# Sums of w_out's blocks split into two parts beside the first gate units and fetched as parts, and one merged block's pooled rows in natural order

## The chip, the cores and the metric

The kernel runs on one core of one Trainium2 chip. Its time is the device time of one execution in microseconds (us); of several runs the median counts. One further execution was profiled, and every duration below comes from that one.

## The reference

One layer of a hybrid encoder block on x of shape (1, 1024, 1024), everything in float32. Cut to what the change touches:

```python
h = rmsnorm(x, norm_mix)
q, k, v, r, lr_f, lr_b, u, g_a, g_b = split(h @ w_in)
o = bidirectional_gated_linear_attention(q, k, v, lr_f, lr_b)      # 4 heads, chunks of 64
y_a = (o * silu(r)) @ w_branch_gla
pooled = multiscale_pool(u)                  # windows 2/4/8/16, mean minus token
y_b = einsum('blgc,gcd->blgd', pooled, w_pool_group) * pool_scale
merged = sigmoid(g_a) * y_a + sigmoid(g_b) * y_b
x = x + merged @ w_out                       # w_out is 1024 x 1024
gate, up = split(rmsnorm(x, norm_ffn) @ w_ffn_in)
x = x + (silu(gate) * up) @ w_ffn_out
return rmsnorm(x, norm_final)
```

## The kernel before

**Arithmetic.** A float32 matrix is held as two parts: a high part, which is a copy rounded to the matmul's input type `fp32r` (`nc.scalar.copy`, on ScalarE: "the cast"), and a low part, the matrix minus its high part (a subtraction on VectorE or GpSimd). A product is three matmuls: high by high, high by low, low by high (`mm3`, the matmuls of L279). The cast with the subtraction is "a split" (`split_to`, L200 and L201). The large matrices are cut in 2 x 2 blocks of 512 and multiplied by a scheme of seven products, p = 1 to 7, in place of eight; some of its factors are blocks and the others are sums or differences of blocks, which other engines form ahead of TensorE. Names end in h and l for the parts: wh/wl of a weight, dh/dl of data.

**Stages.** In order of time: projections and attention (to about 340 us); eleven *gate units* (about 340 to 552), each 256 output columns of w_in times h by seven products of 12 matmuls, of the kinds r (one unit), u (two, the pool input), a and b (four each, the merge gates); the branch product y_a (about 552 to 630); the merged product with w_out (about 630 to 705); the feed-forward stages (to 1318).

**Gate units.** The loop over `gate_runs` runs the unit's products one by one; before each, `gates_ahead.step()` issues what a later product's weights need: a sum of blocks (`fs`, VectorE, L1104), the cast (`wh`, ScalarE, L200) and the subtraction (`wl`, GpSimd, L201). The results are taken from the accumulators by copies on ScalarE (L1492) and adds on VectorE (L1497); for a and b units a sigmoid follows (L1505). For each b unit a small matmul adds the pooling branch (`yb`), and a `scalar_tensor_tensor` on VectorE multiplies it with the gate. The 1024 tokens are held in two halves by parity. The kinds u and r write their rows in natural token order, by reading the accumulator through `sorted_` and writing through `halves`; a and b leave them in the permuted order. a's gates and b's rows go out to HBM (`sa_out`, `yb_out`).

**Work beside the gate units.** `prepare_beside` hangs a generator, `beside`, to the product loop, which advances it by time. Each turn of it does one job in three ages: the job's own operation (`op`, L724), the cast of the job that came `lag` turns earlier (`uph`, L718), and the subtraction of the one cast before that (`upl` on VectorE, L709); a result is written to HBM `put` turns later. At the start of unit 1 it gets `output_jobs`: for each of w_out's four strips of 128 rows it loads the four blocks and forms four differences on GpSimd, which go to `t_wo[p]` in HBM for the products p = 4, 5, 6, 7, unsplit. From unit 8 on it prepares the first two FFN units (`unit_jobs`), whose sums are cast and subtracted there and written as parts (`u_out`). The core of `beside`:

```python
            if differ:
                src, (hi, lo), dst = differ
                nc.vector.tensor_tensor(lo, src, as_f32(hi), op=ALU.subtract)       # L709
            ...
            if cast:
                parts = parts_for(src)
                nc.scalar.copy(parts[0], src)                                       # L718
                differ = src, parts, dst
            ...
                if op:
                    op()                                                            # L724
```

**Branch and merged products.** `line` lists their pieces, two halves c of the inner dimension for each product, with 24 matmuls in a piece. A piece is a triple of functions (`load`, `sums`, `make`): load fetches the raw weights (`wraw`), sums forms the data's sums, make splits data and weights. `project` runs them ahead of the piece that TensorE is at: before each piece it calls `line_load`, `line_make` and `line_sums` once each. The merged products run in the order `MERGED` = 1, 4, 6, 7, 5, 2, 3; in 4, 6, 7 and 5 the weights are the sums from `t_wo`. As the branch products finish, `merge` multiplies their results with the gates and adds the pooled rows (L1624 loads both); for block (1, 1), which comes with branch product 7, that last sum is `padd` on GpSimd (L1639).

**What sets the order.** Every engine runs its instructions in the order written. SyncE issues the loads and stores one after the other, and one that waits for its buffer holds those behind it. Buffers come from pools in turns: six each for wh and wl (`wts`; a piece takes two of each), five for the temporary tiles (`tmp`: the sums' raw strips, uph and upl, the pooling's rows).

Of the kernel before, what the change touches and what calls it, by code (L numbers as in the profile page):

```python
# [10 lines left out]
F32 = mybir.dt.float32  # L11
# [6 lines left out]
P = 128  # L18
# [4 lines left out]
HALF = 512  # L23
# [30 lines left out]
def kernel(  # L54
# [537 lines left out]


    s_out = {p: dram.tile([P, 4, HALF], F32, name=f"s_out{p}") for p in (3, 5, 6, 7)}
    t_wo = {p: dram.tile([P, 4, HALF], F32, name=f"t_wo{p}") for p in (4, 5, 6, 7)}
    READY = 2
    f_order = [f for q in range(PAIRS) for f in (q, q + PAIRS)]
    u_out = [{p: dram.tile([P, 2, HALF], F32, name=f"u_out{n}_{p}") for p in range(1, 8)} for n in range(READY)]
# [31 lines left out]
    def output_jobs(k):  # L630
        (b11, b12, b21, b22), loads = rows_of(w_out, k)
        yield from loads
        for dst, a, b, p in ((b11, b12, b11, 5), (b12, b22, b12, 7), (b22, b22, b11, 6), (b21, b21, b22, 4)):
            yield partial(psub, dst, a, b), None, t_wo[p][:, k, :]

    def unit_jobs(n):
        raw = [slot(F32, (KT, P), "fraw")[:, :, :] for _ in range(2)]
# [653 lines left out]
    def line_load():  # L1291
        if len(loads) < len(line):
            loads.append(line[len(loads)][0]())

    def line_sums():
        if len(begun_sums) < len(line):
            begun_sums.append(line[len(begun_sums)][1]())

    def line_make():
        n = len(made)  # L1300
        if n < len(line):
            while len(loads) <= n:
                line_load()
            if len(begun_sums) <= n:
                while len(begun_sums) <= n:
                    line_sums()
                settle()
            made.append(line[n][2](loads[n]))

    def weight_load(src):  # L1310
        raw = slot(s="wraw")
        nc.sync.dma_start(raw[:, :, :], src)
        return raw

    def weight_split(raw):
        parts = []
# [66 lines left out]
    def merged_piece(p, c):  # L1383
        def load():
            if p in WEIGHT_B:
                i, j = WEIGHT_B[p]
                return weight_load(chunk(w_out, i, j, c))
            return weight_load(t_wo[p][:, 2 * c : 2 * c + 2, :])

        def sums():  # L1390
            def block(i, j):
                return merged[i, j][c][:, :, :]

            if p == 6:
                s3s.append(slot(s="s3"))
                sub(s3s[c][:, :, :], block(0, 0), block(1, 0))
                padd(block(1, 0), block(1, 0), block(1, 1))
                soon(4, partial(sub, block(0, 0), block(1, 0), block(0, 0)))
            elif p == 3:
                sub(block(0, 1), block(0, 1), block(0, 0))  # L1400

        def make(raw):
            a = s3s[c] if p == 7 else merged[{1: (0, 0), 6: (0, 0), 5: (1, 0), 4: (1, 1), 2: (0, 1), 3: (0, 1)}[p]][c]
            return data_split(a, 3.5 if p == 3 else 2), weight_split(raw)

        return load, sums, make

    line += [merged_piece(p, c) for p in MERGED for c in range(2)]

# [53 lines left out]
    class Gates:  # L1463
# [7 lines left out]
        def row(self, i):  # L1471
            while len(self.rows) <= i:
                self.rows.append(slot(s="ga"))
            return self.rows[i]

        def run(self, p):
            while len(right.get(p, ())) < 2:
                next(aside[0][0])
            ps = bank_of(self, p)
            product(self.unit, p, ps, right)  # L1480
            ps = ps[:, :]
            if self.kind in "ur":
                ps = sorted_(ps)
            finish_late()

            def row(i, half):
                t = self.row(i)[:, half, :]
                return halves(t) if self.kind in "ur" else t

            part = {1: (0, 0), 6: (0, 1), 5: (1, 1)}.get(p)  # L1490
            if part:
                nc.scalar.copy(row(*part), ps)  # L1492
                return
            i, half = {2: (0, 0), 3: (0, 1), 4: (1, 0), 7: (1, 1)}[p]
            done = row(i, half)
            if p != 4:
                add(done, ps, done)  # L1497
                ps = done
            if self.kind == "r":
                if p == 4:  # L1500
                    nc.scalar.copy(done, ps)
                late.append(partial(gated, KT - 2 + i, half, done))
                return
            if self.kind != "u":
                nc.scalar.activation(done, ps, AF.Sigmoid)  # L1505
            elif p == 4:
                nc.scalar.copy(done, ps)
            self.done.append((i, half))
            if self.kind == "b" and p in (7, 4):
                for at in self.done:  # L1510
                    self.pooling(*at)
                self.done = []

        def pooling(self, i, half):
            yb = bank(ps_g, "yb")
            mm3(
                yb[:, :], tuple(t[:, i * P : (i + 1) * P] for t in wpool[self.at]),
                tuple(t[:, half, :] for t in pools[self.at]), True, True,
            )
            j, row = 2 * self.at + i, self.row(i)[:, half, :]  # L1520
            late.append(partial(
                nc.vector.scalar_tensor_tensor, row, yb[:, :], g_pool[:, j : j + 1], row, op0=ALU.mult, op1=ALU.mult
            ))

        def store(self, i):
# [14 lines left out]
    for n, run in enumerate(gate_runs):  # L1540
        zs[n] = Gates(n)
        last = n == len(gate_units) - 1
        if n == 1:
            prepare_beside(map(output_jobs, range(4)), 2.8)
        if n == 8:
            finish_side()
            finish_beside()
            prepare_beside(map(unit_jobs, range(READY)), 2.8, 0, 2)
        for at, (of, p) in enumerate(run):
            if not gates_ahead.step() and at in (5, 7):  # L1550
                line_make()
            zs[of].run(p)
            for _ in range(2 * (at == 0 < n and not last)):
                gunits[n + 1].load()
            if p in (7, 4):
                zs[of].store(int(p == 4))
            if at == 4:
                flush()
                if n == 3:
                    begin(pooling(), 4)  # L1560
            if 6 <= n < 10 and at == 5:
                load_pool_weights(n - 6)
            elif n >= 7 and at == 2:
                split_pool_weights(n - 7)
            if n >= 7 and at == (0 if last else 2):
                load_pooled(n - 7)
            if last and at == 1:
                finish_beside()
                load_block(0, 0)
                line_load()  # L1570
                line_load()
                load_block(1, 0)
            elif last and at == 2:
                line_load()
                line_load()
                load_block(0, 1)
                load_block(1, 1)
# [6 lines left out]
    def project(base, products, collect, before, amid=None, first=FIRST, up=UP, pools_of=lambda p: U_BANKS if p == 1 else X_BANKS):  # L1584
        banks = {}
        for at, p in enumerate(products):
            before(p)
            if p in first:
                banks[p in up] = [bank(pool) for pool in pools_of(p)]
            sums = banks[p in up]  # L1590
            for c in range(2):
                n = base + 2 * at + c
                settle()
                while len(made) <= n:
                    line_make()
                    settle()
                line_load()
                line_make()
                line_sums()
                if c == 1 and amid:  # L1600
                    amid(p)
                a, b = made[n]
                for m in range(4):
                    for k in range(2):
                        mm3(
                            sums[m][:, :], tuple(t[:, m * P : (m + 1) * P] for t in a[k]), b[k],
                            c == 0 and k == 0 and p in first, c == 1 and k == 1, p not in first,
                        )
                    if c == 1:
                        collect(p, m, sums[m][:, :])  # L1610
# [17 lines left out]
    def merge(i, j, m, ps, s):  # L1628

        if m == 0:  # L1630
            merged[j, i] = [slot(s="mg") for _ in range(2)]
        dst = quarter(merged[j, i], m)
        sa, yb = (quarter(t, m) for t in gates[i, j])

        if (i, j) == (1, 1):
            dst = halves(dst)
            add(dst, sorted_(ps), sorted_(s))
            nc.vector.tensor_tensor(dst, dst, sorted_(sa), op=ALU.mult)
            padd(dst, dst, sorted_(yb))  # L1639
            return  # L1640
        if s is not None:
            add(ps, ps, s)
        nc.vector.tensor_tensor(ps, ps, sa, op=ALU.mult)
        add(halves(dst), sorted_(ps), sorted_(yb))
# [511 lines left out]
```

## Time and profile before

| what | us |
| --- | --- |
| median of 3 runs | 1325.61 |
| the three runs | 1326.76, 1325.61, 1324.41 |
| the profiled execution | 1323.53 |
| its span (first to last instruction) | 1321.8 |
| TensorE's granted clock, share of full speed | 0.999 |

The busy time of each engine by stage in that execution, from the view by windows:

| from, to (us) | stage | TensorE | VectorE | ScalarE | GpSimd | DMA share | GB/s |
| --- | --- | --- | --- | --- | --- | --- | --- |
| 340.0 to 366.5 | first gate units | 25.82 | 20.60 | 14.57 | 16.22 | 0.76 | 244 |
| 366.5 to 416.3 | gate units beside w_out's sums | 49.80 | 18.22 | 19.22 | 47.77 | 0.79 | 262 |
| 416.3 to 552.0 | the other gate units | 135.70 | 101.67 | 68.33 | 83.97 | 0.81 | 268 |
| 552.0 to 629.7 | branch products | 75.93 | 64.90 | 41.23 | 59.57 | 0.85 | 324 |
| 629.7 to 705.5 | merged products | 73.52 | 59.43 | 37.50 | 51.99 | 0.34 | 117 |

In the profile's rows PE is TensorE (PEld its weight loads), DVE VectorE, ACT ScalarE, POOL GpSimd, SP SyncE. A row of the timeline reads: start, duration, engine, line, operation, result<-operands, and in brackets the idle time before it with what ended it. Matmuls are pipelined, so that their durations overlap; where TensorE stands is read from the distance of their starts. A group of instructions in a row is marked x and its count, and its duration is that of the whole group.

### The profile page before, as it was taken

The numbers are of one execution on the slowest core, as the hardware profiler recorded it, in microseconds if no ns is written. First come the engines' busy times: TensorE is split into PE (matmuls) and PEld (weight loads), VectorE is DVE, ScalarE is ACT, GpSimd is POOL, SyncE is SP. The second block draws the span as 40 slices with busy tenths as digits, with TensorE's granted clock in tenths as the row PEclk, the third lists the DMA queues.
The fourth block names the chain that finished last, engine by engine and source line by source line (L and its number), as shares of the span: only waits on it lengthen the run. The fifth ranks groups of instructions, "written<-read, shape, count | busy, mean of one in ns | idle before, by whom it ended". The sixth has DMA issues, their size and how long they took to land. (4 is left out here: it accounts for less than half of the span.)

```text
span 1321.8 us, 17901 instructions
## 1 busy us (share of the span) xinstructions
PE 1302.2 (99%) x6310; PEld 1138.0 (86%) x6310; DVE 838.3 (63%) x1034; ACT 645.3 (49%) x1177; POOL 769.0 (58%) x557
## 2 busy tenths in 40 slices
PE   9999999999999999999999999999999999999998
PEld 7888888899888888888888888888888888888886
DVE  6975556554735876778884856566666657354375
ACT  7366766665534545554347633333333334454353
POOL 3332734132598657669675286777766778465454
PEclk9999999999999999999999999999999999999999
DMA  7231623134778678996516355555444457995562
GB/s 236 104 104 42 198 75 117 59 101 128 239 247 283 195 223 303 380 409 212 185 65 240 127 189 186 183 183 173 155 142 159 150 160 257 382 349 201 182 223 80
DMA packets 167835, 251.97 MB, mean 191 GB/s; under 512 B 11161, under 2 KB 94145, under 8 KB 167745
## 3 DMA queue, kind: packets, MB, share of 16 engines
q1 hardware_dynamic: 167600, 250.57, 55.8%
q8 instruction: 49, 0.80, 0.3%
q14 instruction: 42, 0.34, 0.1%
q10 hardware_dynamic: 144, 0.26, 0.1%
HBM read 168.74 MB, written 82.05 MB: 190 GB/s over the span
## 5 line engine op out<-in xcount | busy, mean ns | idle before, releaser
L201 POOL TENSOR_TENSOR wl<-fs,wh 128x512 fp32r<-128x512 f32 x124 | 190.7, 1543 | 138.8 <-ACT wh L200 80.9
L279 PE MATMUL ps<-gh,wh 128*128 128x512 f32 x616 | 234.4, 381 | 0.5 <-DVE sums L1880 0.3
L279 PE MATMUL ps<-gl,wh 128*128 128x512 f32 x616 | 233.6, 379 | 0.7 <-DVE gl L1713 0.7
L279 PE MATMUL ps<-gh,wl 128*128 128x512 f32 x616 | 233.5, 379 | 0.0
L201 POOL TENSOR_TENSOR wl<-fraw,wh 128x512 fp32r<-128x512 f32 x93 | 131.1, 1410 | 58.0 <-ACT wh L200 52.8
L201 POOL TENSOR_TENSOR ol<-gor,oh 128x1024 fp32r<-128x1024 f32 (+1 forms) x42 | 103.2, 2462 | 76.0 <-ACT oh L200 63.1
L279 PE MATMUL ps<-hh,wh 128*128 128x512 f32 x356 | 141.1, 396 | 0.7 <-ACT ga L1492 0.7
L279 PE MATMUL ps<-hh,wl 128*128 128x512 f32 x356 | 134.9, 379 | 0.0
L279 PE MATMUL ps<-hl,wh 128*128 128x512 f32 x356 | 134.9, 379 | 0.0
L279 PEld LDWEIGHTS ps<-gh,wh 128*128 128x128 f32 x616 | 116.5, 189 | 17.9 <-DVE sums L1880 0.7
L279 PEld LDWEIGHTS ps<-gl,wh 128*128 128x128 f32 x616 | 116.4, 189 | 17.4 <-DVE gl L1713 1.1
L279 PEld LDWEIGHTS ps<-gh,wl 128*128 128x128 f32 x616 | 116.4, 189 | 16.5
L279 PE MATMUL ps<-oh,oh 128*128 128x512 f32 x308 | 116.8, 379 | 0.2 <-DVE g L1886 0.2
L279 PE MATMUL ps<-ol,oh 128*128 128x512 f32 x308 | 116.7, 379 | 0.0
L279 PE MATMUL ps<-oh,ol 128*128 128x512 f32 x308 | 116.7, 379 | 0.0
L201 POOL TENSOR_TENSOR wl<-wraw,wh 128x512 fp32r<-128x512 f32 x56 | 91.4, 1663 | 38.3 <-ACT wh L200 36.2
L201 POOL TENSOR_TENSOR wl<-raw,wh 128x512 fp32r<-128x512 f32 x34 | 47.0, 1392 | 103.2 <-ACT wh L200 70.3
L201 DVE TENSOR_TENSOR ol<-wor,oh 128x1024 fp32r<-128x1024 f32 (+1 forms) x42 | 66.6, 1601 | 62.6 <-ACT oh L200 55.1
L200 ACT CAST wh<-fs 128x512 fp32r<-128x512 f32 x124 | 75.8, 612 | 25.7 <-DVE fs L1104 23.8
L279 PEld LDWEIGHTS ps<-hh,wl 128*128 128x128 f32 x356 | 67.3, 189 | 9.6
L279 PEld LDWEIGHTS ps<-hh,wh 128*128 128x128 f32 x356 | 67.4, 189 | 9.3 <-ACT ga L1492 1.1
L279 PEld LDWEIGHTS ps<-hl,wh 128*128 128x128 f32 x356 | 67.4, 189 | 8.4
(281 smaller groups left out, 3059.4 us busy)
## 6 DMA issues: line engine op xcount, KB each, us to landing
fraw<-in_w_ffn_in_dram SPq DMA_DIRECT2D x44, 512.0 KB, 5.9
gor<-g_out SPq DMA_DIRECT2D x35, 512.0 KB, 5.7
fraw<-in_w_in_dram SPq DMA_DIRECT2D x22, 512.0 KB, 6.1
g_out<-s SPq DMA_DIRECT2D x44, 256.0 KB, 2.4
wor<-t_out SPq DMA_DIRECT2D x20, 512.0 KB, 4.2
raw<-in_w_in_dram SPq DMA_DIRECT2D x36, 256.0 KB, 5.2
g_out<-g SPq DMA_DIRECT2D x33, 256.0 KB, 2.6
x<-in_x_dram SPq DMA_DIRECT2D x16, 512.0 KB, 5.2
```

What stands on the lines that cost most here:

```text
L200: nc.scalar.copy(hi, src)
L201: eng.tensor_tensor(lo, src, as_f32(hi), op=ALU.subtract)
L279: nc.tensor.matmul(ps.rearrange("p (c a) -> p c a", a=2), a, b.rearrange("p (a c) -> p c a", a=2), **flags)
```

## The change

Three parts:

1. The sums of w_out's blocks are split where they are made. `output_jobs` now hands `beside` the sum as something to cast: behind each of the 16 sums on GpSimd come a cast on ScalarE (L718) and a subtraction on VectorE (L709), and both parts are written to `t_wo`, whose tiles have room for two. That makes 32 writes of 256 KB in place of 16. The call takes `put` = 0: a turn's writes are issued at its end, not three turns later; `lag` stays 1.
2. Merged products 4, 6, 7 and 5 fetch the parts: `line_fetch` and `weight_parts` load each piece's two wh and two wl tiles straight from `t_wo`, 32 loads of 256 KB in place of 8 of 512 KB into wraw, 16 casts on ScalarE and 16 subtractions on GpSimd. The fetch of a piece is called behind the make of the piece before it, where the raw load of before stood four pieces ahead.
3. The rows that `merge` adds in block (1, 1) are kept in natural token order. A new method `sorts` says which rows are so written: those of the kinds u and r as before, and half 0 of the units b with at >= 2. Their four evacuations and the multiplications with `yb` read through `sorted_` and write through `halves`, and the `padd` in `merge` reads the rows contiguously.

```diff
-    t_wo = {p: dram.tile([P, 4, HALF], F32, name=f"t_wo{p}") for p in (4, 5, 6, 7)}
+    t_wo = {p: dram.tile([P, 4, 2, HALF], F32, name=f"t_wo{p}") for p in (4, 5, 6, 7)}
...
-            yield partial(psub, dst, a, b), None, t_wo[p][:, k, :]
+            yield partial(psub, dst, a, b), dst, t_wo[p][:, k]
...
+    fetched = {}
+
+    def line_fetch():
+        n = len(made)
+        if n < len(line) and n not in fetched and line[n][3:]:
+            fetched[n] = line[n][3]()
...
-            made.append(line[n][2](loads[n]))
+            line_fetch()
+            made.append(line[n][2](fetched.get(n) or loads[n]))
...
+    def weight_parts(src):
+        parts = [wts.tile([P, HALF], F32R, tag=s, name=name(s))[:, :] for s in ("wh", "wl")]
+        for i, t in enumerate(parts):
+            nc.sync.dma_start(as_f32(t), src[:, i, :])
+        return parts
...
-            return weight_load(t_wo[p][:, 2 * c : 2 * c + 2, :])
...
-            return data_split(a, 3.5 if p == 3 else 2), weight_split(raw)
+            return data_split(a, 3.5 if p == 3 else 2), weight_split(raw) if p in WEIGHT_B else raw
+
+        def fetch():
+            return [weight_parts(t_wo[p][:, 2 * c + k]) for k in range(2)]
 
-        return load, sums, make
+        return (load, sums, make) if p in WEIGHT_B else (load, sums, make, fetch)
...
+        def sorts(self, half):
+            return self.kind in "ur" or self.kind == "b" and half == 0 and self.at >= 2
...
-            if self.kind in "ur":
-                ps = sorted_(ps)
...
-                return halves(t) if self.kind in "ur" else t
+                return halves(t) if self.sorts(half) else t
 
             part = {1: (0, 0), 6: (0, 1), 5: (1, 1)}.get(p)
+            i, half = part or {2: (0, 0), 3: (0, 1), 4: (1, 0), 7: (1, 1)}[p]
+            if self.sorts(half):
+                ps = sorted_(ps)
...
-            j, row = 2 * self.at + i, self.row(i)[:, half, :]
+            j, row, yb = 2 * self.at + i, self.row(i)[:, half, :], yb[:, :]
+            if self.sorts(half):
+                row, yb = halves(row), sorted_(yb)
             late.append(partial(
-                nc.vector.scalar_tensor_tensor, row, yb[:, :], g_pool[:, j : j + 1], row, op0=ALU.mult, op1=ALU.mult
+                nc.vector.scalar_tensor_tensor, row, yb, g_pool[:, j : j + 1], row, op0=ALU.mult, op1=ALU.mult
...
-            prepare_beside(map(output_jobs, range(4)), 2.8)
+            prepare_beside(map(output_jobs, range(4)), 2.8, 0)
...
                 line_make()
+                line_fetch()
                 line_sums()
...
-            padd(dst, dst, sorted_(yb))
+            padd(dst, dst, halves(yb))
```

The order of TensorE's instructions stays as it was. Three places where another engine's order changes follow; the numbers behind the names count tiles, and differ between the two kernels, as the line numbers do (L1516 and L1524 of the changed kernel are L1497 and L1505 of before).

ScalarE, in the gate units, at the last of w_out's four strips (wsum are the strip's tiles, ga the gates' rows, fraw and fs raw gate weights and their sums). Before:

```order
L200 CAST wh_4191<-fraw_4124 128x512
L1505 ACT_TABLE_LOAD
L1505 ACTIVATE ga_4122<-ga_4122 128x512
L200 CAST wh_4216<-fs_4195 128x512
L1505 ACTIVATE ga_4122<-ga_4122 128x512
L200 CAST wh_4244<-fs_4220 128x512
```

With the change:

```order
L200 CAST wh_4251<-fraw_4178 128x512
L718 CAST uph_4261<-wsum_4193 128x512
L718 CAST uph_4275<-wsum_4193 128x512
L1524 ACT_TABLE_LOAD
L1524 ACTIVATE ga_4176<-ga_4176 128x512
L200 CAST wh_4285<-fs_4255 128x512
L718 CAST uph_4301<-wsum_4194 128x512
L1524 ACTIVATE ga_4176<-ga_4176 128x512
L200 CAST wh_4318<-fs_4289 128x512
L718 CAST uph_4329<-wsum_4194 128x512
```

Four casts stand among the sigmoids and the gate weights' casts, each behind a sum on GpSimd; the two of wsum_4193 stand ahead of the activation table.

VectorE at the same place, with the change (without the upl rows it is the order of before; ps are accumulators):

```order
L709 TENSOR_TENSOR upl_4276<-wsum_4193,uph_4275 128x512
L1516 TENSOR_TENSOR ga_4176<-ps_4186,ga_4176 128x512
L709 TENSOR_TENSOR upl_4302<-wsum_4194,uph_4301 128x512
L709 TENSOR_TENSOR upl_4330<-wsum_4194,uph_4329 128x512
L1516 TENSOR_TENSOR ga_4209<-ps_4156,ga_4209 128x512
L1104 TENSOR_TENSOR fs_4349<-fraw_4178,fs_4289 128x512
```

Two subtractions stand ahead of an add that empties an accumulator.

SyncE's loads from the start of the merged products on (t_wo_543 belongs to product 4, t_wo_545 to product 6; x are the residual's rows). Before:

```order
L1665 DMA x_1269_6195<-in_x_dram 128x1024
L1312 DMA wraw_6197<-t_wo_543 128x1024
L1312 DMA wraw_6235<-t_wo_543 128x1024
L1312 DMA wraw_6299<-t_wo_545 128x1024
L1312 DMA wraw_6337<-t_wo_545 128x1024
L1665 DMA x_1305_6383<-in_x_dram 128x1024
```

With the change:

```order
L1326 DMA wh_6422<-t_wo_545 128x512
L1326 DMA wl_6423<-t_wo_545 128x512
L1326 DMA wh_6426<-t_wo_545 128x512
L1326 DMA wl_6427<-t_wo_545 128x512
L1687 DMA x_1337_6463<-in_x_dram 128x1024
L1687 DMA x_1338_6465<-in_x_dram 128x1024
L1687 DMA x_1339_6467<-in_x_dram 128x1024
L1687 DMA x_1340_6469<-in_x_dram 128x1024
L1326 DMA wh_6478<-t_wo_545 128x512
L1326 DMA wl_6479<-t_wo_545 128x512
```

The raw loads become four loads of parts for a piece, with the residual's rows between the fetches of two pieces of product 6.

More of the change, by code (lines that the diff above doesn't have):

```diff
@@ L1493, in run @@
                 return
-            i, half = {2: (0, 0), 3: (0, 1), 4: (1, 0), 7: (1, 1)}[p]
             done = row(i, half)
```

## The prediction

> **What bounds the kernel now.** I read the page first, then who TensorE waits for in the stages that the change touches, then the timeline around those waits.
>
> ```profile
> span 1321.8 us, 17901 instructions
> PE 1302.2 (99%) x6310; PEld 1138.0 (86%) x6310; DVE 838.3 (63%) x1034; ACT 645.3 (49%) x1177; POOL 769.0 (58%) x557
> ```
>
> TensorE is busy for 1302.2 of 1321.8 us and the change leaves its matmuls alone, so only the 19.6 us in which it stands can be won. Seen from 340 to 760 us, this is its longest wait:
>
> ```profile
> PE ps L279 <- POOL wl L201: 2.7, 4, 1.4
> ```
>
> Four waits on the low parts of weights. The timeline (start, duration, instruction, idle before it) shows where:
>
> ```profile
> 618.05 0.38 PE L279 MATMUL ps<-dl,wh 128*128 128x512 f32 x1
> 619.05 0.48 PE L279 MATMUL ps<-dh,wl 128*128 128x512 f32 x1 [0.62 <-POOL wl L201]
> 619.37 0.38 PE L279 MATMUL ps<-dh,wh 128*128 128x512 f32 x1
> 619.59 0.38 PE L279 MATMUL ps<-dl,wh 128*128 128x512 f32 x1
> 620.28 0.48 PE L279 MATMUL ps<-dh,wl 128*128 128x512 f32 x1 [0.32 <-POOL wl L201]
> ...
> 655.35 0.38 PE L279 MATMUL ps<-wh,dl 128*128 128x512 f32 x1
> 655.73 0.48 PE L279 MATMUL ps<-wh,dh 128*128 128x512 f32 x1
> 657.60 0.48 PE L279 MATMUL ps<-wl,dh 128*128 128x512 f32 x1 [1.39 <-POOL wl L201]
> ...
> 658.14 0.38 PE L279 MATMUL ps<-wh,dh 128*128 128x512 f32 x1
> 658.84 0.48 PE L279 MATMUL ps<-wl,dh 128*128 128x512 f32 x1 [0.33 <-POOL wl L201]
> ```
>
> Matmuls start 0.22 us apart (619.37 to 619.59). Against that step, 618.05 to 619.05 loses 0.78 us, 619.59 to 620.28 0.47, and the slow start behind each 0.10 (619.05 to 619.37): **1.45 us** at 618, where the branch weights of product 4 are late. At 655, in piece 1 of merged product 6, whose weights are sums of w_out blocks, 0.16 + 1.65 + 0.10 + 0.48 + 0.10 = **2.5 us**. The kernel has no other stall that the change addresses.
>
> **Merged products: 16 casts and 16 subtractions go.** GpSimd and VectorE ahead of the second stall:
>
> ```profile
> 649.47 3.35 POOL L1397 TENSOR_TENSOR mg<-mg,mg 128x1024 f32<-128x1024 f32 x1
> 655.76 17.02 POOL L201 TENSOR_TENSOR wl<-wraw,wh 128x512 fp32r<-128x512 f32 x10 [2.94 <-ACT wh L200]
> 655.19 1.22 DVE L165 TENSOR_TENSOR dl<-mg,dh 128x1024 fp32r<-128x1024 f32 x1 [1.11 <-ACT dh L1327]
> ```
>
> The late wl is the first of ten at 655.76. With product 6 fetched as parts, that wait is gone. Next in line is the data: its low part ends at 656.41, and the third matmul wants it at 655.73 + 0.44 = 656.17, so 0.24 us at most would come back. It will also come earlier, since the sum on GpSimd (649.47) no longer stands behind weight splits. I take the whole 2.5 us, with 2.2 as the low end.
>
> The fetch itself is not seen before; the nearest row is the same shape fetched for the first FFN units, beside the writes of such parts and of the plain sums (KB, median us to landing):
>
> ```profile
> wh<-u_out SPq DMA_DIRECT2D x14, 256.0 KB, 3.7
> u_out<-uph SPq DMA_DIRECT2D x14, 256.0 KB, 3.5
> t_wo<-wsum SPq DMA_DIRECT2D x16, 256.0 KB, 4.5
> ```
>
> wh and wl have six buffers each, three pieces, so a piece's four DMAs wait on SyncE for the piece three earlier to leave TensorE. From there two pieces of 24 matmuls, 2 x 24 x 0.216 = 10.4 us, pass before it is wanted; with 3.7 us of landing that holds as long as the four issues take under 6.7 us together. Cost: nothing. Behind the waiting fetches stand the second four x rows, the last four raw pieces of w_out and the first FFN weights; all are wanted at least two products later.
>
> **Natural order of the pooled rows: nothing.** The GpSimd sum reads one operand at every second element now, and contiguously after. Its rows, with the splits before it and VectorE's neighbours:
>
> ```profile
> 605.67 1.91 POOL L201 TENSOR_TENSOR wl<-wraw,wh 128x512 fp32r<-128x512 f32 x1
> 607.54 1.91 POOL L1639 TENSOR_TENSOR mg<-mg,gate 128x512 f32<-128x512 f32 x1
> 611.33 4.19 POOL L1639 TENSOR_TENSOR mg<-mg,gate 128x512 f32<-128x512 f32 x1
> ...
> 612.01 1.21 DVE L1355 TENSOR_TENSOR ob<-ob,t 128x1024 f32<-128x1024 f32 x1
> 613.14 1.20 DVE L165 TENSOR_TENSOR dl<-ob,dh 128x1024 fp32r<-128x1024 f32 x1
> 614.38 2.22 DVE L165 TENSOR_TENSOR dl<-ob,dh 128x1024 fp32r<-128x1024 f32 x1
> ```
>
> A contiguous split and the strided sum take 1.91 us alike. The 4.19 us are no stride: VectorE ran two instructions with two SBUF inputs at 1.2 us each, GpSimd stood, and then the third took 2.22, about one GpSimd instruction longer. The two engines take turns. [...] So the stall at 618 stays: 0 of its 1.45 us, at best all of them. In the gate units the permuted access moves to four products, whose evacuations form the u units already use.
>
> **Gate units: what is added.** 16 casts on ScalarE, 16 subtractions on VectorE, 16 more writes, between 366 and 416 us. Busy time there (all engines, then of lines L201, L724 and L1104):
>
> ```profile
> 366.50:416.30 49.80, 49.80 (x235) 43.61 (x234) 18.22 (x21) 19.22 (x34) 47.77 (x37) 1.00 0.79 262
> ...
> 366.50:416.30 49.80, 0.00 (x0) 25.94 (x19) 1.00 0.79 262
> ...
> 366.50:416.30 49.80, 0.00 (x0) 22.50 (x16) 1.00 0.79 262
> ...
> 366.50:416.30 49.80, 11.83 (x11) 1.00 0.79 262
> L709 DVE TENSOR_TENSOR upl<-fraw,uph x14: 679/898/1762, 500.4 to 536.6; 128x512 fp32r<-128x512 f32 x14
> ```
>
> ```profile
> POOL wl L201 <- ACT wh L200: 0.8, 1, 0.8
> POOL wsum L724 <- DMA wsum<-in_w_out_dram: 0.5, 1, 0.5
> ```
>
> ScalarE and VectorE have room; **GpSimd is full**: 47.77 of 49.80. Its 19 splits and 16 sums take 48.4 us against 35 x 1.27 = 44.5 alone: the 11 VectorE sums of L1104 cost it 4.0 us by the turns shown above, 0.36 each. Each upl has two SBUF inputs as well and 0.68 us alone, so it costs GpSimd between 0 and 0.6 us. By 0.36, the 12 ahead of the 14th sum cost 4.3 us; GpSimd's gaps in the last two rows (its waits, total, times, longest) give back 1.3. It is then **3.0 us late** (0 to 5.9).
>
> Before, nobody but SyncE waited for these sums. Now ScalarE does, in order, and behind its cast stand the activation table, a sigmoid and the next weights' cast, which TensorE needs. The rows of that place:
>
> ```profile
> 408.27 1.28 ACT L1505 ACT_TABLE_LOAD   x1
> 410.53 0.64 ACT L1505 ACTIVATE ga<-ga 128x512 f32<-128x512 f32 x1 [0.98 <-DVE ga L1497]
> 411.07 0.60 ACT L200 CAST wh<-fs 128x512 fp32r<-128x512 f32 x1
> 417.50 0.59 ACT L1492 COPY ga<-ps 128x512 f32<-128x512 f32 x1 [0.65 <-PE ps L279]
> 420.10 0.59 ACT L1492 COPY ga<-ps 128x512 f32<-128x512 f32 x1
> ...
> 409.56 2.97 POOL L724 TENSOR_TENSOR wsum<-wsum,wsum 128x512 f32<-128x512 f32 x2
> 412.48 1.28 POOL L201 TENSOR_TENSOR wl<-fs,wh 128x512 fp32r<-128x512 f32 x1
> ...
> 414.99 0.69 DVE L1497 TENSOR_TENSOR ga<-ps,ga 128x512 f32<-128x512 f32 x1 [1.90 <-PE ps L279]
> ```
>
> The product that needs this wl starts at 417.5 (the copy behind its predecessor); products are 2.6 us apart. On time, the 14th sum ends at 411.05 (half of 2.97); uph 0.62, table 1.28, sigmoid 0.64, wh 0.60 and wl 1.28 give 415.5, 2.0 us early. With 3.0 us of lag TensorE stands 1.0. Then the add at 414.99: on VectorE it now comes behind the last two upl, and the last waits for a buffer, that is, for the write of the 15th uph to land. On time: wh at 414.2, uph 414.85, landing 3.5, upl 0.68, add 0.69: 419.7, and TensorE adds into that bank at 420.05. 3.0 us of lag make 422.7 against 421.05, another 1.65 us. Gate units lose 1.0 + 1.65, **2.7 us** (0 without lag; with 5.9 of lag and the 4.5 us landing, 6.6). The other weights of these units I take as covered: no table load stands ahead of them. So are the raw gate weights and the pooling's rows, which queue on SyncE behind the new writes: they are loaded about a unit, seven products or 18 us, ahead. The 16 extra writes of 256 KB add 4.2 MB in 50 us to the 262 GB/s of that row, 84 GB/s; what slower landings could cost lies in the 4.5 us above.
>
> **Sum.** -2.5 + 2.7 = +0.2 us on the profiled execution: 1321.8 of span and 1.7 around it, 1323.5, become 1323.7. The median of the runs is 2.1 us above that execution, so 1325.6 becomes **1325.8**: no change.
>
> **Rivals.**
> 1. The lag is hidden. For it: ScalarE and VectorE are under 40% busy here, and 14 uph/upl pairs near 520 us cost TensorE nothing. Against: GpSimd was less full there. Then only -2.5: 1323.1. Chance 0.28.
> 2. Both early stalls go: the sums on GpSimd end sooner after all, by other turns or a stride that does cost. For it: 4.19 us is far above the splits. Against: 1.91 equals 1.91. With the lag hidden, -2.5 - 1.45: 1321.7. Chance 0.14.
> 3. Slower: at 412 to 423 us, GpSimd loses 0.6 us, not 0.36, to each upl; lag 5.9, loss up to 6.6, so +4.1: 1329.7. It decides once the lag passes about 5 us. [...] For it: the rows at 611 to 616; against: the 11 sums cost 0.36. Chance 0.20.
> 4. The parts land late and the wait at 655 comes back as a DMA wait: issue and landing together would have to pass 10.4 us, against a landing of 3.7. That gives back up to 2.5: 1328.3; inside the others' range, 0.04.
>
> My forecast has 0.34, with its own range 1324.3 to 1327.3. The range reaches from rival 2 to most of rival 3: **1321.8 to 1329.2**. A measurement of this kernel can tell about 0.2%, 2.7 us, from no change: faster is rival 2 and nearly half of rival 1 (0.27); slower is rival 3, half of rival 4 and the forecast's edge (0.25); 0.48 between.
>
> **What would show it.** Right: no wait on wl near 655; the wait at 618 still there; new TensorE waits between 412 and 425 us, on wl and on a ga of VectorE; ScalarE idle before uph with GpSimd's sums as releaser. Wrong: TensorE without a gap from 366 to 425 (rival 1), no wait at 618 (rival 2), GpSimd's splits stretched by more than 0.4 us per upl (rival 3), or wh/wl waits on DMA near 640 to 660 (rival 4).

## The result and the profile after

| kernel | median, us | runs | ratio to before (95% interval) |
| --- | --- | --- | --- |
| before | 1325.67 | 1324.41 to 1328.54 (5) | |
| with the change | 1332.07 | 1330.47 to 1336.24 (5) | 1.0052 (1.0035 to 1.0068) |

The change makes the kernel slower by 6.4 us. The forecast was 1325.8, no change, with a range from 1321.8 to 1329.2. From the page of the changed kernel (its profiled execution took 1331.45 us):

```profile
span 1329.7 us, 17977 instructions
PE 1307.5 (98%) x6310; PEld 1140.8 (86%) x6310; DVE 856.6 (64%) x1050; ACT 644.1 (48%) x1177; POOL 744.7 (56%) x541
```

The same 6310 matmuls, in the same order, keep TensorE busy for 5.3 us longer than before, and the granted clock of this execution is 0.995 against 0.999. So two things are to be found: stands (stretches in which TensorE waits), and a slower clock. The two profiled executions are 7.9 us apart in span (1321.8 and 1329.7); that is what the account below is of.

**Where the time went.** The copies that empty accumulators come in the same order in both kernels and serve as marks. From the timeline of before, two of them and a matmul of the FFN's start:

```profile
381.25 0.59 ACT L1492 COPY ga<-ps 128x512 f32<-128x512 f32 x1 [4.72 <-PE ps L279]
438.27 0.58 ACT L1492 COPY ga<-ps 128x512 f32<-128x512 f32 x1 [1.49 <-issue]
729.50 0.38 PE L279 MATMUL ps<-gh,wl 128*128 128x512 f32 x1
```

The same three in the changed kernel:

```profile
381.97 0.59 ACT L1512 COPY ga<-ps 128x512 f32<-128x512 f32 x1 [2.66 <-PE ps L279]
449.42 0.58 ACT L1512 COPY ga<-ps 128x512 f32<-128x512 f32 x1 [0.42 <-ACT wh L200]
737.27 0.38 PE L279 MATMUL ps<-gh,wl 128*128 128x512 f32 x1
```

The lag goes from 0.72 us to 11.15 and back to 7.77: the gate units lose **10.4 us** in one stretch, and the branch and merged products give back 3.4 (2.5 at 655, and 0.4 and 0.5 in the stands at 585 and 618). The timeline of TensorE in that stretch, with the change:

```profile
419.54 0.38 PE L279 MATMUL ps<-hh,wl 128*128 128x512 f32 x1
422.28 0.48 PE L279 MATMUL ps<-trh,wh 128*128 128x512 f32 x1 [2.35 <-ACT wh L200]
422.60 0.38 PE L279 MATMUL ps<-trl,wh 128*128 128x512 f32 x1
423.63 0.80 PE L279 MATMUL ps<-trh,wl 128*128 128x512 f32 x1 [0.65 <-POOL wl L201]
424.22 0.63 PE L279 MATMUL ps<-trh,wh 128*128 128x512 f32 x1
...
427.63 0.63 PE L279 MATMUL ps<-trh,wl 128*128 128x512 f32 x1
428.81 0.80 PE L279 MATMUL ps<-trh,wh 128*128 128x512 f32 x1 [0.55 <-DVE ga L1516]
...
432.81 0.55 PE L279 MATMUL ps<-trh,wh 128*128 128x512 f32 x1
433.20 0.38 PE L279 MATMUL ps<-trl,wh 128*128 128x512 f32 x1
```

The reader is to look at the distance of the starts. At full speed it is 0.22 us; from 424.22 on it is 0.43 (the full list has 424.65, 425.07, 425.50). Behind a stand of 2.5 us and one of 0.8 the matmuls run at half speed until 432.9. The view by windows says so directly (window and its length, TensorE's busy time and matmuls, its clock, then DMA share and GB/s):

```profile
420.00:422.00 2.00, 0.00 (x0) 1.00 1.03 408
422.00:424.00 2.00, 1.07 (x3) 0.73 1.00 306
424.00:426.00 2.00, 2.00 (x6) 0.50 0.88 296
```

The account of the 10.4 us: 2.52 and 0.81 at 419.5 and 422.6, smaller stands of 0.68, 0.31 and 0.41 at 394, 406 and 417, which makes 4.7; then, from 423.63 to 433.20, 20 steps that should take 4.3 us take 9.6. Of these 5.3 us some 1.1 are the stand at 428 and what follows it, and **4.2 are the clock**: 20 x 0.21. Some 0.4 are too small to single out.

**Why the weights were late.** ScalarE, GpSimd and VectorE around that place, with the change:

```profile
419.16 0.62 ACT L718 CAST uph<-wsum 128x512 fp32r<-128x512 f32 x1 [2.29 <-POOL wsum L724]
419.79 1.28 ACT L1524 ACT_TABLE_LOAD   x1
...
421.62 0.60 ACT L200 CAST wh<-fs 128x512 fp32r<-128x512 f32 x1
...
384.96 1.27 POOL L724 TENSOR_TENSOR wsum<-wsum 128x512 f32<-128x512 f32 x1 [2.35 <-DMA wsum<-in_w_out_dram]
414.93 1.28 POOL L724 TENSOR_TENSOR wsum<-wsum 128x512 f32<-128x512 f32 x1 [1.95 <-DMA wsum<-in_w_out_dram]
417.40 3.40 POOL L724 TENSOR_TENSOR wsum<-wsum,wsum 128x512 f32<-128x512 f32 x2
...
427.46 0.69 DVE L709 TENSOR_TENSOR upl<-wsum,uph 128x512 fp32r<-128x512 f32 x1 [3.32 <-DMA t_wo<-uph]
428.07 0.68 DVE L1516 TENSOR_TENSOR ga<-ps,ga 128x512 f32<-128x512 f32 x1
```

The chain on ScalarE is the one that was forecast: cast, table, sigmoid, the weights' cast that TensorE waits for. But the 14th sum begins at 417.40, where before it began at 409.56; taking off TensorE's own lag of 2 us by then, it is nearly 6 us late, not 3.0. And GpSimd, which should have been late by being full alone, also *stands*: twice it waits for a strip of w_out to land, 4.3 us in all. From the split before the first sum (366.55 before, 367.27 now) to the 14th sum it is busy for 44.34 us against 41.10 and idle for 5.79 against 1.91: of 7.1 us of delay 3.9 are waiting, and 3.2 are work that takes longer. SyncE's rows show why the second strip came late:

```profile
370.46 0.34 SPq L732 DMA_DIRECT2D t_wo<-uph  x1
374.74 0.34 SPq L732 DMA_DIRECT2D t_wo<-upl  x1
375.13 0.91 SPq L574 DMA_DIRECT2D ob_out<-o  x2
376.13 0.93 SPq L732 DMA_DIRECT2D t_wo<-uph  x1
377.17 1.15 SPq L732 DMA_DIRECT2D t_wo<-upl  x1
378.40 1.33 SPq L608 DMA_DIRECT2D wsum<-in_w_out_dram  x2
```

From 370.8 to 374.7 SyncE holds on to the write of the first upl, which VectorE has not made yet, and behind that write stand the next ones and the strip's load. Before, that load went out at 374.64:

```profile
374.64 1.40 SPq L608 DMA_DIRECT2D wsum<-in_w_out_dram  x2
...
380.60 1.75 POOL L724 TENSOR_TENSOR wsum<-wsum 128x512 f32<-128x512 f32 x1 [0.54 <-DMA wsum<-in_w_out_dram]
```

The last two rows of VectorE above show a third thing: the subtraction waits for the write of an earlier uph to land, since uph and upl take turns on five tiles, and TensorE's accumulator waits behind it. (Its own data, the last uph, was made by 425.92; the first half of the 3.32 us is the late sum, the rest the tile.)

**The merged products** did as forecast. Between 655 and 735 us the matmuls that read weights, the low parts among them, stand for nothing but 0.2 us (group, count, busy time and mean ns, idle time in front of it):

```profile
L279 PE MATMUL ps<-wh,dh 128*128 128x512 f32 x89 | 34.4, 386 | 0.2 <-DVE x L1826 0.2
L279 PE MATMUL ps<-wl,dh 128*128 128x512 f32 x89 | 33.7, 379 | 0.0
```

### The profile page after: what moved, and what is told of

It is laid out like the page before. It is cut to its first block, busy times and chain, and to the rows that moved or that the text cites. A ratio compares the mean times of both kernels' runs of the same rounds, so it can differ in the third digit from the quotient of the medians.

```text
span 1329.7 us, 17977 instructions
## 1 busy us (share of the span) xinstructions
PE 1307.5 (98%) x6310; PEld 1140.8 (86%) x6310; DVE 856.6 (64%) x1050; ACT 644.1 (48%) x1177; POOL 744.7 (56%) x541
## 5 line engine op out<-in xcount | busy, mean ns | idle before, releaser
L201 POOL TENSOR_TENSOR wl<-wraw,wh 128x512 fp32r<-128x512 f32 x40 | 65.8, 1675 | 49.3 <-ACT wh L200 47.7
```

The source lines that it names most:

```text
L201: eng.tensor_tensor(lo, src, as_f32(hi), op=ALU.subtract)
```

## The experiments

Three causes were now on the table for the lag, each with a way of taking it away: **A**, strips loaded late, since SyncE holds their loads; **B**, GpSimd slowed by turns with the new subtractions, which is the prediction's; **T**, the five temporary tiles. Each ratio is to the kernel before, run on the same chip.

### The natural order alone

> Part 3 alone: the kernel before, with the pooled rows of block (1, 1) in natural order. If the strided operand costs GpSimd time, its four sums fall from 10.2 us together to about 7.8, as in the changed kernel, and the stand near 618 us shrinks from 1.45 us by 0.5 to 1.45: 1324.2 to 1325.2. If the long third sum was only a matter of turns with VectorE, as the prediction has it, the stand stays at 1.45 and the time at 1325.7. Either way no new stand in the gate units: the loss of the changed kernel isn't here.

```diff
-            if self.kind in "ur":
+            if self.sorts(half):
...
-            padd(dst, dst, sorted_(yb))
+            padd(dst, dst, halves(yb))
```

1325.52 us, ratio 1.0001 (0.9992 to 1.0010). GpSimd's four sums, in one row of the timeline, do get shorter than the 10.2 us (607.54 to 617.72) of before:

```profile
609.57 7.83 POOL L1644 TENSOR_TENSOR mg<-mg,gate 128x512 f32<-128x512 f32 x4
```

The stand at 618 falls from 1.45 to about 1.0 us, but the one at 585 (on VectorE's dl) is 1.4 rather than 1.0, and one of 0.6 is new at 536. So GpSimd's four sums are 2.4 us shorter, and the time shows none of it. Nearly 2 us of that are one sum: the single sums lasted 1.91 to 4.19 us before and 1.90 to 2.26 here, so the shortest are alike, and the long one stood beside VectorE's instructions. Whether the stride by itself costs anything is not shown.

### The strips loaded earlier

> The changed kernel, with each of w_out's strips 2 to 4 loaded at the first sum of the strip before it, so that on SyncE its load stands ahead of that strip's writes and not behind two to four of them. Theory A (the strips come late, since SyncE holds their loads behind writes that wait for casts and subtractions): GpSimd's waits for the strips, 4.3 us in all, go; the sums come 4 us earlier or more; the stands between 382 and 432 us fall from 6.4 us to under 3, TensorE's clock stays whole, and the time falls from 1332.1 to 1324 to 1326. Theory B (GpSimd is late by its turns with the new subtractions, as the prediction has it): the sums stay 3 to 6 us late, the stands and the clock's loss stay: 1330 or more.

```diff
+        for n, (dst, a, b, p) in enumerate(...):
+            def op(...):
+                if n == 0 and k < 3:
+                    strip_load(k + 1)
+                psub(dst, a, b)
+            yield op, dst, t_wo[p][:, k]
```

1329.44 us, ratio 1.0032 (1.0020 to 1.0045): 2.6 us back, between the two expectations. GpSimd's waits for strips are gone, the small stands at 394 and 406 too, but the 14th sum still comes at 414.3, and stands of 1.62, 0.81 and 2.81 us stay. A is real, and not all. The longest stand has VectorE's rows in front of it:

```profile
424.26 0.69 DVE L724 TENSOR_TENSOR upl<-wsum,uph 128x512 fp32r<-128x512 f32 x1 [3.20 <-DMA t_wo<-uph]
424.87 0.68 DVE L1531 TENSOR_TENSOR ga<-ps,ga 128x512 f32<-128x512 f32 x1
```

### The casts a turn later

> The changed kernel with the casts two turns behind their sums, not one (some 2.8 us later), as the FFN units' preparation has it. ScalarE then finds sums that are up to 3 us late already made. By theory B (lag of 3.0 us) the stands at 417 to 429 us go: 1323 to 1325. By theory A the lag is 6 us and comes from the loads, which now stand behind one pair of writes rather than two: about half of the stands stay, and the clock drops only if one of them is still over 2 us: 1325 to 1329.

```diff
-            prepare_beside(map(output_jobs, range(4)), 2.8, 0)
+            prepare_beside(map(output_jobs, range(4)), 2.8, 0, 2)
```

1332.27 us, ratio 1.0056 (1.0043 to 1.0068): both expectations miss. VectorE waits for tiles five times (4.96, 2.47, 6.17, 0.98 and 3.50 us before an upl), and TensorE stands 1.72 us at 384 and 3.0 at 426 behind those. What a later cast wins on ScalarE is lost to T. It shows the clock once more:

```profile
425.98 0.63 PE L279 MATMUL ps<-trh,wl 128*128 128x512 f32 x1
429.20 0.48 PE L279 MATMUL ps<-trh,wh 128*128 128x512 f32 x1 [2.59 <-DVE ga L1516]
...
430.17 0.62 PE L279 MATMUL ps<-trl,wh 128*128 128x512 f32 x1
...
433.57 0.39 PE L279 MATMUL ps<-trh,wh 128*128 128x512 f32 x1
```

Half speed before the stand (starts 0.43 us apart), full speed behind it for 0.9 us (0.22), half again from 430.1 to 433.5. The first drop, at about 423.3, came behind stands of 1.64 and 1.10 us, so that the 2 us of the expectation are not the limit; no run shows one.

### The sums three units later

> The changed kernel with w_out's sums begun at gate unit 4 in place of 1, where GpSimd is busy 84 of 136 us and not 48 of 50, and the pooling is under way. By theory A and B alike GpSimd has room to be late there, and ScalarE waits less for it; the merged products keep their gain of some 3 us: 1322 to 1323. If it is rather the five temporary buffers, shared there with the pooling's rows, that hold the casts, stands of over 1 us appear between 412 and 490 us and the time is 1325 or more.

```diff
-        if n == 1:
+        if n == 4:
             prepare_beside(map(output_jobs, range(4)), 2.8, 0)
```

1366.55 us, ratio 1.0314 (1.0300 to 1.0329), 41 us slower: the second expectation (1325 or more), and far worse than it had in mind. There the pooling's rows take turns on the same five tiles. From the view of waits, 430 to 520 us:

```profile
PE ps L279 <- DVE ga L1516: 19.8, 2, 11.2
DVE upl L709 <- DMA t_wo<-uph: 12.1, 2, 6.8
```

Waits for tiles are among the longest, but GpSimd and ScalarE wait long for each other there as well; that the tiles account for the whole 41 us was not tested.

### A sixth temporary tile

> The changed kernel with six temporary tiles in place of five (and four of the small tiles, to make room). Theory T (the casts and subtractions wait for one of five tiles, until the write of an earlier part has landed): those waits, 2.8 us on ScalarE near 392 us and 4.8 us on VectorE at 423 to 427 us, mostly go, and with them the stand on VectorE's add (1.3 us at 428) and part of the clock's loss; the stand on late weights at 419 to 423 (3.3 us) stays, since the strips still come late: 1327 to 1330. If the tiles don't matter: 1332.

```diff
-    tmp = ctx.enter_context(tc.tile_pool(name="tmp", bufs=5))
-    small = ctx.enter_context(tc.tile_pool(name="small", bufs=5))
+    tmp = ctx.enter_context(tc.tile_pool(name="tmp", bufs=6))
+    small = ctx.enter_context(tc.tile_pool(name="small", bufs=4))
```

1327.34 us, ratio 1.0014 (1.0005 to 1.0024): 4.7 us back. The stand on VectorE's add is gone and half speed lasts 3 us rather than 9; the stand on late weights (2.51 us) stays, as does GpSimd's wait for two strips.

> The changed kernel with four small tiles in place of five and the five temporary tiles kept: the room made in the runs with six tiles, without its use. If what those runs gained (4.7, 4.75 and 5.6 us) comes from the sixth tile, this one stays at 1332 or above, with VectorE's waits for the write of an uph as in the changed kernel. If the smaller set of small tiles itself moved something, it falls below 1330.

1331.73 us, ratio 1.0046 (1.0029 to 1.0062). So it is the sixth tile.

### The sums on VectorE

> The changed kernel with the 16 sums on VectorE in place of GpSimd, which then has 25 of 50 us to do. Theory B (GpSimd, full and slowed by turns, is late with the sums and splits): the splits come on time and most of the stands go: 1323 to 1327. Theory A (the strips' loads are late): the sums wait for them on VectorE as they did on GpSimd, now ahead of the adds that empty the accumulators, so the stands stay or grow: 1331 or more.

```diff
-            yield partial(psub, dst, a, b), dst, t_wo[p][:, k]
+            yield partial(sub, dst, a, b), dst, t_wo[p][:, k]
```

1331.13 us, ratio 1.0041 (1.0026 to 1.0056), not to be told from the changed kernel's 1332.07. The stands stay: VectorE now waits 4.20 us for the last strip, at 413.5.

> Both: strips loaded at the first sum of the strip before, and the sums on VectorE. If A and B between them hold the whole loss, the stands between 382 and 432 us are under 1 us together, the clock stays whole, and the merged products' gain of 3 us is left: 1322 to 1323.5. If theory T has a part of its own, VectorE still waits for temporary tiles there and a stand of 1 to 3 us remains: 1324 to 1328.

1326.51 us, ratio 1.0009 (1.0000 to 1.0018). The stands on weights are gone; one of 3.75 us on VectorE's add is left, behind an upl that waited 2.72 us for a tile. That is T by itself.

### Two taken away, then all three

> Two of the three taken away: strips loaded early (A) and six temporary tiles (T); GpSimd still makes the sums. If A and T each hold what their single runs gave back (2.6 and 4.7 of the 7 us), the stand on VectorE's add behind the last subtractions (2.81 us in the run with early loads) goes, and what is left is theory B's: GpSimd full at 410 to 416 us, ScalarE's cast waiting for the 14th sum, one stand of 1.6 + 0.8 us at 417 to 420 and no drop of the clock: 1324 to 1325.5. If nothing of B is left either: 1322 to 1323.

1324.69 us, ratio 0.9995 (0.9985 to 1.0004). This is the prediction's world: nothing waits for strips, and only GpSimd is late. Its rows:

```profile
412.95 3.42 POOL L648 TENSOR_TENSOR wsum<-wsum,wsum 128x512 f32<-128x512 f32 x2
417.88 1.28 POOL L201 TENSOR_TENSOR wl<-fs,wh 128x512 fp32r<-128x512 f32 x1 [1.50 <-ACT wh L200]
```

The 14th sum begins 3.4 us later than before (409.56; TensorE's own lag is nothing by then), and TensorE stands 0.57 and 0.81 us on the weights and 1.87 on VectorE's add, 3.25 in all, without a drop of the clock.

> All three taken away: strips early, six temporary tiles, the sums on VectorE. By A + B + T no stand over 0.7 us between 382 and 432 us, the clock whole, and the merged products' gain left: 1321 to 1323. If there is a fourth cause (VectorE, now with 32 more operations, itself late), a stand on its add stays: 1324 or more.

1320.90 us, ratio 0.9964 (0.9950 to 0.9978). No stand over 0.4 us is left between 355 and 618 us. In the 49.8 us window GpSimd (last busy time) does half of its former work, VectorE the more:

```profile
366.50:416.30 49.80, 49.80 (x235) 43.61 (x234) 42.33 (x50) 26.68 (x48) 26.28 (x18) 1.00 0.89 304
```

The medians of these runs, in us (the kernel before had 1325.0 to 1325.7 beside them):

| | GpSimd sums | VectorE sums |
| --- | --- | --- |
| as changed | 1332.07 | 1331.13 |
| strips early | 1329.44 | 1326.51 |
| six tiles | 1327.34 | not run |
| strips early, six tiles | 1324.69 | 1320.90 |

Each cause was taken away from more than one start: A gives 2.6, 2.65 and 4.6 us, T 4.75, 4.7 and 5.6, B 0.9, 2.9 and 3.8. The 0.9 lies within the spread of the runs. B here means that GpSimd has too much to do: the move takes whole sums off it, and not only the turns with the subtractions. The three do not add up as independent terms, for one late instruction hides behind another, and the clock adds its part by steps (1.00 or 0.50 in the changed kernel's windows of 0.2 us, but for the two in which it changes, with 0.77 and 0.63).

### Product 6 alone

> The changed kernel with the sums of merged product 6 alone as parts: 4 casts and 4 subtractions beside the gate units in place of 16, those of products 4, 7 and 5 written and fetched raw as before, and writes three turns late again. The wait near 655 us goes as in the changed kernel (2.5 us). By A, B and T alike the gate units lose under 0.5 us: 4 x 0.36 = 1.4 us of GpSimd's time against its 1.3 us of gaps, and eight fewer tiles in use at a time. 1322 to 1323.5. If a stand comes back at product 7 or 5, whose weights are split on GpSimd again, the gain halves: 1324.

```diff
+            if p in PARTED:                 # PARTED = (6,)
+                yield partial(psub, dst, a, b), dst, t_wo[p][:, k]
+            else:
+                yield partial(psub, dst, a, b), None, t_wo[p][:, k, :]
...
-            prepare_beside(map(output_jobs, range(4)), 2.8, 0)
+            prepare_beside(map(output_jobs, range(4)), 2.8)
```

1321.12 us, ratio 0.9968 (0.9956 to 0.9979), faster than both kernels by 4.3 and 11 us. Only one stand before named a product of the merged stage, and only that product's weights are prepared ahead; the writes go out three turns later again, as before. The stand at 655 is gone here too. The 14th sum is on time again (410.25, with TensorE 0.7 later there by itself):

```profile
410.25 2.96 POOL L728 TENSOR_TENSOR wsum<-wsum,wsum 128x512 f32<-128x512 f32 x2
```

The profiled execution is 2.3 us shorter than that of before (span 1319.5 against 1321.8), which the stand at 655 explains; the other 2 us of the medians have no place in the traces. And all sixteen parts with the writes three turns late were not run, so how much of the loss goes back to the earlier writes alone is open.

> Product 6 alone as parts, without the natural order of the pooled rows. If the natural order is worth nothing in the sum, as its run alone has it (1.0001), the time stays at 1321.1 and the stand near 619 us is 1.2 to 1.5 us rather than 0.9. If the 0.5 us at that stand come through: 1321.6 to 1322.

1321.96 us, ratio 0.9971 (0.9959 to 0.9982): the natural order changes nothing that these runs can tell. The stand at 618 is 0.78 + 0.48 us without it, 0.90 with it.

## Why the prediction was wrong

- **The merged products: right.** The 2.5 us at 655 are gone, and no wait on a fetched part took their place. The four fetches of a piece came in time, also past the residual's rows.
- **Natural order, nothing: right in the sum, and the reading stays open.** The four sums fell from 10.2 to 7.8 us, but most of that is the one sum of 4.19 us, which the prediction gave to the turns with VectorE, and the shortest sums are alike (1.91 and 1.90). The stand at 618 shrank by 0.4 us, which no median shows.
- **The place and the chain of the loss: right.** TensorE waits on the weights behind ScalarE's cast of the 14th sum, then on VectorE's add behind the last subtractions, at 419 to 428 us.
- **The lag of 3.0 us: right for its cause, and not the lag that ruled.** With A and T taken away GpSimd is 3.4 us late and TensorE stands 3.25 us, against 3.0 and 2.7 forecast. GpSimd's 30 instructions ahead of the 14th sum took 45.47 us there against 41.10 before: 4.4 us for 12 subtractions, the 0.36 us each of the estimate; the rival with 0.6, a lag of 5.9 us, did not hold, though the time it gave (1329.7) is the nearest to the measured one. That the two engines take turns is the prediction's reading of its rows and not shown as such. What the run with both other causes away shows is that VectorE's subtractions (upl) take from 0.68 to 1.77 us beside GpSimd, while its adds that read an accumulator (L1531) take 0.68 each.
- **The first step that failed** is the sentence that called the loads behind the new writes on SyncE covered. It named the raw gate weights and the pooling's rows, about a unit ahead, and left out the strips themselves, which are loaded three turns before their first sum (6 us in the trace of before: 374.64 to 380.60), on the same queue. With the writes put out in their own turn, SyncE waits for cast and subtraction in front of the next strip's load. That is A: the second strip's load went out 3.8 us later (378.40 against 374.64, of which 0.7 are TensorE's lag), and GpSimd stood for it. Loading ahead of the writes gave back 2.6 to 4.6 us.
- **The second step that failed: the wait for a tile was counted once**, for the last subtraction behind the write of the 15th uph, and as part of a chain that starts from the sum. It held ScalarE before that too (0.53 us at 394, ahead of the stand there), and its price in the runs (T, 4.7 to 5.6 us) is larger than the whole forecast loss. The stands at 394 and 406 (1.0 us), on ScalarE's copies behind waiting casts, had no term in the sum. With A alone taken away the time is 1329.44, with T alone 1327.34, with both 1324.69, 1.1 us below the forecast: it takes both.
- **The third: a stand was priced at its own length.** Two stands of 3.3 us together cost 4.2 us more by the clock. Neither the sum nor a rival had that term; the stands alone, some 6 us, would have put the time near 1328, within the range, and by luck, since their causes were not those of the prediction.

## What to carry to other kernels

When a write is moved closer to the instruction that makes its data, look at what the issuing queue has behind it: here the next load of the very same job was late. A buffer that stays in use longer is a cost like an instruction, and it is read by counting who takes turns on its pool until the last reader's write has landed. Prepare ahead only what the profile shows to be late: four of the sixteen sums (1321.12 us) gave as much here as all sixteen did with the three causes taken away (1320.90), while all sixteen as the change had them, with the earlier writes, cost 11 us more.

## What the runs showed of the hardware

- TensorE's clock went to half behind stands that were each shorter than 2.6 us: after 2.52 + 0.81 us here, after 1.64 + 1.10 at 419 to 422 us with the casts a turn later. It stayed whole after 1.65 + 0.48 us at 655 (before), and after 0.57, 0.81 and 1.87 us spread over 6 us (strips early, six tiles). Half speed lasted about 3.4 us (430.1 to 433.5, with the casts a turn later); in the changed kernel the clock column, in steps of 0.2 us, has it from 422.9 to 433.1, some 10.2 us, three times that. A further stand fell into it; whether that is why is not shown.
- A stand of 3.18 us, longer than any of these, left the clock whole (behind it the starts are 0.22 us apart from 501.38 to 505.70), with the sums three units later:

```profile
497.66 0.38 PE L279 MATMUL ps<-trl,wh 128*128 128x512 f32 x1
501.06 0.48 PE L279 MATMUL ps<-trh,wl 128*128 128x512 f32 x1 [3.02 <-POOL wl L201]
```

- Two more runs show half speed of about that length, read from the starts: 424.0 to 427.4 us with six tiles, behind 2.51 and 0.81 us, and 425.6 to 429.0 with strips early, behind 2.81, where 1.62 and 0.81 at 417 to 420 had left the clock whole. The length of a stand does not decide alone: 3.18 us left the clock whole, 1.64 and 1.10 did not. What decides is not shown.
- GpSimd and VectorE beside each other: from 366 to 416 us before the change, VectorE's nine adds that read an accumulator (L1497) took 0.69 us each, and its eleven sums with both inputs in SBUF (L1104) 0.68 to 1.76. With natural order, in the changed kernel, GpSimd's four sums took 2.4 us less, while VectorE's instruction beside them, also with two inputs in SBUF, took 2.30 us in place of 1.21 (L1369 at 622.60, and L1355 at 612.01 before). What makes one longer beside the other is not shown.
